# Three operations of VectorE issued later in the order: a weight sum, a product of norm weights, and the transposes of the keys

## The chip, the core and the metric

The kernel runs on one core of one Trainium2 chip. The core has TensorE (PE, the matrix engine; PEld is its weight load), VectorE (DVE), ScalarE (ACT), GpSimd (POOL) and SyncE (SP, which here only issues transfers), and DMA engines that move data between HBM and SBUF. Each engine works through one queue of instructions in order; an instruction that waits holds up everything behind it in its queue. The metric is the device time of one execution in microseconds (us), as the median of several runs.

## What is computed

The reference is a decoder trunk of two layers on 256 tokens with model width 2048 and feed-forward width 8192. Layer 0 mixes tokens with gated linear attention, layer 1 with sliding-window attention over keys and values that are computed once between the layers. Both layers end in an MLP with a squared ReLU.

```python
def sqrelu_mlp(h, w1, w2):
    u = jax.nn.relu(h @ w1)
    return (u * u) @ w2

def shared_kv(h, g_kv, w_k, w_v, g_k):
    u = rmsnorm(h, g_kv)
    k = rmsnorm((u @ w_k).reshape(B, S, SWA_KV_HEADS, SWA_HEAD_DIM), g_k)
    v = (u @ w_v).reshape(B, S, SWA_KV_HEADS, SWA_HEAD_DIM)
...
def swa_sink_mixer(h, k_band, v_band, w_q, g_q, sinks, w_o):
    q = (h @ w_q).reshape(B, S, SWA_KV_HEADS, SWA_GROUP, SWA_HEAD_DIM)
    q = rmsnorm(q, g_q) * (SWA_HEAD_DIM ** -0.5)
```

The keys' norm weight `kv_g_k` and the queries' norm weight `b_g_q` only ever meet as a product, which the kernel forms once (`gkq`) and multiplies into the keys.

## The kernel before

**Matrix products.** Every float32 operand is split into two halves: a rounded half (`wh` for weights, made by ScalarE, line 116) and the rest (`wl`, made by VectorE as `ws - wh`, line 117). A product of a 128x128 block is three matmuls: high by high, high by low, low by high. The function `halve` makes four `wh`/`wl` k-blocks of a 512x512 weight piece in two ScalarE and two VectorE instructions of 128x1024. There are four buffers of `wh` (two k-blocks each), three of `wl` and three of `ws`, the landing place of a weight piece of 1 MB. VectorE comes after ScalarE for each half, and TensorE after VectorE.

**The order of the queues.** The kernel is written as a program in one order; the compiler fills each engine's queue. An instruction's number is its place in the program, and of the instructions that are ready an engine gets the one with the lowest number. `tc.high_priority(offset=WPRI)` gives an instruction a number 60 lower, so that weight loads, halves and weight sums move ahead of their place. The helpers `later(n, fn)` and `tick()` are a clock in the program: `fn` is written n ticks later, and a tick passes about every 12 matmuls.

**The MLP's second product.** For three or four of the four groups of hidden columns (g), `seven` (line 712) computes two times two blocks of 512 columns with Strassen-like sums: seven products in place of eight. It runs for n = 0 and n = 1 in each of seven groups, thus 14 times. The steps that matter here, with the lines:

- `x` and `y` are weight blocks in buffers of their own (783, 791). `y` is block (1,1).
- `plain(2, 1, "E", "F")` (790) multiplies the block (2,1) into two accumulation banks, E for the first 128 tokens and F for the second. Both banks come from the pool `ms`, which has two. At n = 0 they were last used by the first product (`gemm_wide`), whose sums are read out in lines 838 and 839; line 843 applies the ReLU, 844 squares, 847 and 848 split the result.
- `product("E", 2, y)` (792) halves `y` and multiplies.
- Lines 793 to 795 load block (0,1) as `b12` and add it to `y` on VectorE: the last weight sum of the quarter.
- `plain(3, 1, "E", "F")` (796), the sums of E and F into `x12` and `x22` (797, 798), `product("D", 4, x)` (799), a transfer that accumulates onto `x` (`more`, 800, issued by GpSimd), a sum (801).
- `product("C", 6, y)` (802) halves the summed `y` and multiplies: the first user of the sum.
- `plain` of the blocks (2,0) and (3,0), `product("D", 5, x)`, and then in the same manner `b21` added to `x` in line 813.

**Between the layers.** When the last MLP columns of layer 0 are done, four groups of transposes (`operands`, line 614; PE line 610) turn the residual stream into the operands of the key/value product and the query product, with ScalarE in line 241 and VectorE in line 242; `rstd_of` (644) sums the squares. They are written at ticks 0 to 3 around the start of the key/value product. GpSimd meanwhile makes masks (885 to 898) and fetches the two norm weights into `gk` (903, 904). VectorE multiplies them into `gkq` (906). The key/value product (950) is 96 matmuls with a tick after every 12. Its result is normalised (`evac_kv`, 934), multiplied by `gkq` (942), split in two halves (945, 946), and 16 transposes on TensorE with four ScalarE copies (`flip`, 926) bring the keys into `kh` and `kl`; these are written 2 and 3 ticks after the key/value product's end, among the first query product's matmuls (1056).

Of the kernel before, what the change touches and what calls it, by code (L numbers as in the profile page):

```python
# [12 lines left out]
ALU = mybir.AluOpType  # L13
# [18 lines left out]
HD = 64  # L32
NEG = -1.0e30
WS = 3
WHL = 4
WPRI = 60
# [12 lines left out]
def yoco_kernel(ctx: ExitStack, tc: tile.TileContext, x, norms, mlp_w1, mlp_w2, a_w_in, w_glr, w_gate, a_g_o, a_w_o,  # L49
                kv_w_k, kv_w_v, kv_g_k, b_w_q, b_g_q, b_sinks, b_w_o, out):  # L50
    nc = tc.nc
# [4 lines left out]
    wp = ctx.enter_context(tc.tile_pool(name="wp", bufs=2))  # L56
# [14 lines left out]
    def later(n, fn):  # L71
        due.setdefault(now[0] + n, []).append(fn)

    def tick():
        now[0] += 1
        for fn in due.pop(now[0], ()):
            fn()

    def mm(o, l, r, start=True, stop=True, **kw):
        nc.tensor.matmul(o, lhsT=l, rhs=r, start=start, stop=stop, **kw)  # L80
# [23 lines left out]
    def halve(ws, o=C, n=2, between=None):  # L104

        whs = [wp.tile([P, 2, C], F32R, name="wh", tag="wh", bufs=WHL) for _ in range(2)]
        wl = wp.tile([P, 4, C], F32R, name="wl", tag="wl", bufs=WS)
        with tc.high_priority(offset=WPRI):
            for k in range(0, 4, n):
                wh = whs[k // 2]  # L110
                js, ks = slice(k % 2, k % 2 + n), slice(k, k + n)
                with ExitStack() as order:
                    if between:
                        for ins in between(k):
                            order.enter_context(tc.issue_after(ins.ins))
                    h = nc.scalar.copy(out=wh[:, js, :o], in_=ws[:, ks, :o])  # L116
                    l = nc.vector.tensor_sub(out=wl[:, ks, :o], in0=ws[:, ks, :o], in1=wh.bitcast(F32)[:, js, :o])  # L117
                if between:
                    last[:] = h, l
        return [(whs[k // 2][:, k % 2], wl[:, k]) for k in range(4)]  # L120
# [550 lines left out]
    def mlp(w1, w2, act, r, gains):  # L671
# [40 lines left out]
        def seven(w, n, op, us, g, final, acts, gains, sq, nr):  # L712
# [6 lines left out]
            def block(i, j):  # L719
                return w[i * C:(i + 1) * C, (c0 + j) * C:(c0 + j + 1) * C]  # L720

            def load(pool, tag, bufs, i, j):
                ws = pool.tile([P, 4, C], F32, name=tag, tag=tag, bufs=bufs)
                with tc.high_priority(offset=WPRI):
                    nc.sync.dma_start(out=ws, in_=block(i, j).rearrange("(k p) n -> p k n", p=P))
                return ws

            def more(ws, i, j):
                with tc.high_priority(offset=WPRI):
                    nc.gpsimd.dma_start(out=ws, in_=block(i, j).rearrange("(k p) n -> p k n", p=P), accum_op=ALU.add)  # L730
# [3 lines left out]
            def use(b):  # L734
                if b in banks:
                    return banks[b], False
                banks[b] = bank([P, C], {"D": "tp", "E": "ms", "F": "ms"}.get(b, "acc"))
                return banks[b], True

            def product(b, o, ws):  # L740
                p, st = use(b)
                halves = halve(ws)
                for k in range(4):
                    wh, wl = halves[k]
                    mm(p, op[o][:, 0, k], wh, st and k == 0, False, skip_group_check=True)
                    mm(p, op[o][:, 0, k], wl, False, False, skip_group_check=True)
                    mm(p, op[o][:, 1, k], wh, False, k == 3, skip_group_check=True)
                tick()
                return p

            def plain(i, j, b0, b1, apart=False):

                halves = split_w([block(i, j)])
                ah, al, _ = us[i]
                ps_ = [use(b) for b in (b0, b1)]
                order = [(k, t) for k in range(4) for t in range(NT)]
                for n, (k, t) in enumerate(sorted(order, key=lambda kt: kt[1]) if apart else order):
                    wh, wl = halves[k]
                    p, st = ps_[t]
                    tt = slice(t * P, (t + 1) * P)  # L760
                    mm(p, ah[:, k, tt], wh, st and k == 0, False, skip_group_check=True)
                    mm(p, ah[:, k, tt], wl, False, False, skip_group_check=True)
                    mm(p, al[:, k, tt], wh, False, k == 3, skip_group_check=True)
                    if n % 4 == 3:
                        tick()
# [18 lines left out]
            p = product("A", 0, x)  # L784
# [5 lines left out]
            plain(2, 1, "E", "F")  # L790
            y = load(mp, "wy", 1, 1, 1)
            product("E", 2, y)
            b12 = load(wp, "ws", WS, 0, 1)
            with tc.high_priority(offset=WPRI):
                nc.vector.tensor_add(out=y, in0=y, in1=b12)  # L795
            plain(3, 1, "E", "F")
            add(x12, banks["E"])
            add(x22, banks["F"])
            p = product("D", 4, x)
            more(x, 1, 1)  # L800
            add(x21, p)
            sub(x22, product("C", 6, y))
            for i in (2, 3):
                plain(i, 0, "A", "C", i == 2)
# [67 lines left out]
    def last_x(c, b, mp):  # L872

        if b == 0:
# [27 lines left out]
    gk = sp.tile([P, 2, HD], F32, name="gk")  # L902
    nc.gpsimd.dma_start(out=gk[:, 0], in_=kv_g_k.rearrange("(o n) -> o n", o=1).broadcast_to([P, HD]))
    nc.gpsimd.dma_start(out=gk[:, 1], in_=b_g_q.broadcast_to([P, HD]))
    gkq = sp.tile([P, 1, HD], F32, name="gkq")
    nc.vector.scalar_tensor_tensor(out=gkq[:, 0], in0=gk[:, 0], scalar=HD ** -0.5, in1=gk[:, 1], op0=ALU.mult,
                                   op1=ALU.mult)

    def rows(m, n):
        return m.rearrange("p (o n) -> p o n", o=1).broadcast_to([P, n, P])  # L910
# [15 lines left out]
    def flip(src, n, dst):  # L926

        for i in range(0, n, 4):
            tp = bank([P, 4, P], "tp", F32R)
            for j in range(4):  # L930
                nc.tensor.transpose(out=tp[:, j, :], in_=src(i + j), identity=identr)  # L931
            nc.scalar.copy(out=dst(i), in_=tp.bitcast(F32))

    def evac_kv(t, acc):
        a = acc.rearrange("p (h d) -> p h d", d=HD)
        rq = head_norm(a[:, 0:4], 4, t)
        rq = rq.rearrange("p (n o) -> p n o", o=1).broadcast_to([P, 4, HD])
        kn = s2.tile([P, 4, 1, HD], F32, name="kn", tag="kn")
        nc.vector.scalar_tensor_tensor(out=kn[:, :, 0], in0=a[:, 0:4], scalar=rstd[:, t:t + 1], in1=rq, op0=ALU.mult,
                                       op1=ALU.mult)  # L940
        nc.scalar.activation(out=vv[:, t], in_=a[:, 4:8], func=AF.Copy, scale=rstd[:, t:t + 1])
        nc.vector.tensor_mul(out=kn[:, :, 0], in0=kn[:, :, 0], in1=gkq.broadcast_to([P, 4, HD]))
        khl = s2.tile([P, 2, 4, 2, HD], F32R, name="khl", tag="qhl")
        kn2 = kn.broadcast_to([P, 4, 2, HD])
        nc.scalar.copy(out=khl[:, 0], in_=kn2)
        nc.vector.tensor_sub(out=khl[:, 1], in0=kn2, in1=khl.bitcast(F32)[:, 0])
        later(2 + t, lambda: flip(lambda i: khl[:, i // 4, i % 4].rearrange("p a d -> p (a d)"), 8,
                                  lambda i: (kh, kl)[i // 4][:, :, t]))

    go_all(gemm_mov(lambda kq: [kv_w_k[kq * C:(kq + 1) * C, :], kv_w_v[kq * C:(kq + 1) * C, :]], actk, evac_kv))  # L950
# [154 lines left out]
```

## Time and profile before

| | |
|---|---|
| median of 3 runs | 2090.39 us (2089.78 to 2093.33) |
| profiled execution, own time | 2090.28 us |
| its span, first to last instruction | 2088.6 us |
| mean granted TensorE clock | 0.997 |
| VectorE busy | 1428.7 us, 1624 instructions |
| ScalarE busy | 1146.7 us, 1560 instructions |
| GpSimd busy | 177.0 us, 179 instructions |

How to read it: a row of the timeline is a start in us, a duration, the engine, the line, the operation, what it writes and reads, and the number of instructions merged; in square brackets stands how long the engine sat idle before and what ended it. Durations overlap a little with the next instruction, so the distance of two starts is what an instruction costs in a full queue. Of the windows, the last columns are the granted TensorE clock as a share of full speed, the share of the DMA engines, and GB/s. In the view of waits the columns are total us, times, and the longest.

### The profile page before, as it was taken

The page shows a single profiled execution, that of the slowest core. Times are in us where ns is not written, and L with a number is a line of the kernel's source. Part 1 is how long each engine was busy: PE and PEld are TensorE (multiplying, and loading weights), DVE is VectorE, ACT ScalarE, POOL GpSimd, SP SyncE. Part 2 cuts the span into 40 slices and gives each one's busy share as a digit, 9 for nine tenths or more (in the row PEclk, how much of TensorE's full clock was granted, in tenths as well). Part 3 has the DMA queues.
Part 4 walks back from the last instruction along what each step waited for, and adds up shares of the span by engine and source line. Part 5 has one row for each costly group of instructions (what it writes and reads, how often), then busy time and mean ns, then how long its engine had stood idle before and what let it go on. Part 6 is the DMA issues. An engine that isn't in the chain of part 4 may idle for free.

```text
span 2088.6 us, 26959 instructions
## 1 busy us (share of the span) xinstructions
PE 2056.3 (98%) x10734; PEld 1738.8 (83%) x10734; DVE 1428.7 (68%) x1624; ACT 1146.7 (55%) x1560; POOL 177.0 (8%) x179
## 2 busy tenths in 40 slices
PE   9999999999999999999999999999999999999999
PEld 8988888888888788888877777788788888888888
DVE  6696444567866876786797666656776786787554
ACT  6745445555655555554565676455555555555543
POOL 2262111000000000000001232000000000000000
PEclk9999999999999999999999999999999999999999
DMA  8445555656865785776675443655785686676553
GB/s 278 142 142 180 175 174 176 230 190 189 242 231 189 211 270 184 213 240 213 199 193 157 158 141 112 221 188 185 208 271 184 190 255 222 182 225 198 182 192 130
DMA packets 210654, 410.55 MB, mean 197 GB/s; under 512 B 7024, under 2 KB 15232, under 8 KB 210528
## 3 DMA queue, kind: packets, MB, share of 16 engines
q1 hardware_dynamic: 194704, 377.51, 53.8%
q0 software_dynamic: 15104, 30.23, 8.4%
q8 instruction: 84, 1.38, 0.3%
q10 hardware_dynamic: 720, 1.09, 0.2%
q14 instruction: 42, 0.34, 0.0%
HBM read 406.71 MB, written 2.10 MB: 196 GB/s over the span
## 4 chain that ended last, share of the span: by engine, by line
PE 88%; DVE 7%; ACT 3%; issue 1%; DMA 1%; POOL 0%; SPq 0%; ACTq 0%; POOLq 0%; DVEq 0%
PE acc L80 55%; PE ms L80 19%; PE tp L80 13%; DVE wl L117 3%; ACT sc L998 1%; ACT wh L116 1%; PE tp L610 1%; DVE wy L795 1%; DVE m L839 0%; PE tp L931 0%; DVE st L992 0%; DMA ws<-in_a_w_in_dram 0%; DVE st L994 0%; DMA gk<-in_b_g_q_dram 0%; PE tp L559 0%
## 5 line engine op out<-in xcount | busy, mean ns | idle before, releaser
L117 DVE TENSOR_TENSOR wl<-ws,wh 128x1024 fp32r<-128x1024 f32 (+1 forms) x636 | 780.0, 1234 | 472.5 <-ACT wh L116 467.7
L116 ACT CAST wh<-ws 128x1024 fp32r<-128x1024 f32 (+1 forms) x636 | 659.4, 1040 | 577.0 <-PE acc L80 387.6
L80 PE MATMUL acc<-wh,act 128*128 128x512 f32 x1792 | 575.5, 395 | 0.1
L80 PE MATMUL acc<-act,wh 128*128 128x512 f32 (+1 forms) x1664 | 414.1, 362 | 2.2 <-ACT wh L116 1.4
L80 PEld LDWEIGHTS acc<-wh,act 128*128 128x128 f32 x1792 | 336.2, 188 | 73.0 <-issue 3.6
L80 PE MATMUL acc<-wl,act 128*128 128x512 f32 x896 | 349.8, 391 | 0.0
L80 PEld LDWEIGHTS acc<-act,wh 128*128 128x128 f32 x1664 | 278.9, 190 | 29.7 <-ACT wh L116 1.6
L80 PE MATMUL acc<-act,wl 128*128 128x256 f32 x1408 | 257.6, 282 | 0.6 <-DVE wl L117 0.6
L80 PEld LDWEIGHTS acc<-act,wl 128*128 128x128 f32 x1408 | 227.0, 190 | 26.2 <-DVE wl L117 1.0
L80 PE MATMUL tp<-act,wh 128*128 128x512 f32 x592 | 230.1, 394 | 0.0
L80 PE MATMUL ms<-act,wh 128*128 128x512 f32 x576 | 225.9, 394 | 0.0
L80 PEld LDWEIGHTS acc<-wl,act 128*128 128x128 f32 x896 | 168.8, 188 | 35.3 <-issue 1.7
L117 DVE TENSOR_TENSOR wl<-wx,wh 128x1024 fp32r<-128x1024 f32 x112 | 135.9, 1223 | 73.1 <-ACT wh L116 71.2
L116 ACT CAST wh<-wx 128x1024 fp32r<-128x1024 f32 x112 | 117.7, 1055 | 94.3 <-PE acc L80 52.4
L80 PE MATMUL ms<-act,wl 128*128 128x256 f32 x576 | 148.6, 281 | 0.0
L80 PE MATMUL tp<-act,wl 128*128 128x256 f32 x576 | 148.3, 280 | 0.0
L80 PE MATMUL ms<-wh,act 128*128 128x512 f32 x448 | 146.0, 394 | 0.9
L730 POOL DMA_DIRECT2D wx<-in_mlp_w_dram x28 | 36.1, 1289 | 1128.4 <-DVE wl L117 1026.7
L80 PEld LDWEIGHTS tp<-act,wh 128*128 128x128 f32 x592 | 111.5, 189 | 13.3
L80 PEld LDWEIGHTS ms<-act,wh 128*128 128x128 f32 x576 | 108.6, 189 | 13.6
L80 PEld LDWEIGHTS tp<-act,wl 128*128 128x128 f32 x576 | 108.3, 189 | 12.7
L80 PEld LDWEIGHTS ms<-act,wl 128*128 128x128 f32 x576 | 108.5, 189 | 11.9
(231 smaller groups left out, 2242.9 us busy)
## 6 DMA issues: line engine op xcount, KB each, us to landing
ws<-in_mlp_w_dram SPq DMA_DIRECT2D x228, 1024.0 KB, 5.2
ws<-in_a_w_in_dram SPq DMA_DIRECT2D x44, 1024.0 KB, 5.1
wx<-in_mlp_w_dram POOLq DMA_DIRECT2D x28, 1024.0 KB, 8.9
ws<-in_a_w_o_dram SPq DMA_DIRECT2D x16, 1024.0 KB, 5.0
ws<-in_b_w_q_dram SPq DMA_DIRECT2D x16, 1024.0 KB, 5.0
ws<-in_b_w_o_dram SPq DMA_DIRECT2D x16, 1024.0 KB, 5.0
wx<-in_mlp_w_dram SPq DMA_DIRECT2D x14, 1024.0 KB, 5.1
wy<-in_mlp_w_dram SPq DMA_DIRECT2D x14, 1024.0 KB, 7.5
```

Source lines behind the costliest of these rows:

```text
L80: nc.tensor.matmul(o, lhsT=l, rhs=r, start=start, stop=stop, **kw)
L116: h = nc.scalar.copy(out=wh[:, js, :o], in_=ws[:, ks, :o])
L117: l = nc.vector.tensor_sub(out=wl[:, ks, :o], in0=ws[:, ks, :o], in1=wh.bitcast(F32)[:, js, :o])
L610: nc.tensor.transpose(out=tp[:, j, t], in_=xs[c][:, t, (2 * b + j) * P:(2 * b + j + 1) * P], identity=ident)
L730: nc.gpsimd.dma_start(out=ws, in_=block(i, j).rearrange("(k p) n -> p k n", p=P), accum_op=ALU.add)
L795: nc.vector.tensor_add(out=y, in0=y, in1=b12)
L998: nc.scalar.activation(out=sc[:, h], in_=sc[:, h], func=AF.Exp, bias=nmx[:, h:h + 1], scale=f[:, h:h + 1], accum_out=su[:, h:h + 1])
```

## The change

Three places are written later in the program; no instruction is added, removed or made different.

- In `seven`, the load of `b12` and its sum into `y` move from before `plain(3, 1)` to just before `product("C", 6, y)`: behind 36 matmuls, two sums and the halves of two weight pieces in the written order, still with the 60 of `WPRI`.
- `gkq` is written at the fourth tick of the key/value product instead of before it.
- The keys' transposes are written 5 and 6 ticks after the key/value product instead of 2 and 3.

```diff
             y = load(mp, "wy", 1, 1, 1)
             product("E", 2, y)
-            b12 = load(wp, "ws", WS, 0, 1)
-            with tc.high_priority(offset=WPRI):
-                nc.vector.tensor_add(out=y, in0=y, in1=b12)
             plain(3, 1, "E", "F")
             add(x12, banks["E"])
             add(x22, banks["F"])
             p = product("D", 4, x)
             more(x, 1, 1)
             add(x21, p)
+            b12 = load(wp, "ws", WS, 0, 1)
+            with tc.high_priority(offset=WPRI):
+                nc.vector.tensor_add(out=y, in0=y, in1=b12)
             sub(x22, product("C", 6, y))
...
     gkq = sp.tile([P, 1, HD], F32, name="gkq")
-    nc.vector.scalar_tensor_tensor(out=gkq[:, 0], in0=gk[:, 0], scalar=HD ** -0.5, in1=gk[:, 1], op0=ALU.mult,
-                                   op1=ALU.mult)
+    later(4, lambda: nc.vector.scalar_tensor_tensor(out=gkq[:, 0], in0=gk[:, 0], scalar=HD ** -0.5, in1=gk[:, 1],
+                                                    op0=ALU.mult, op1=ALU.mult))
...
-        later(2 + t, lambda: flip(lambda i: khl[:, i // 4, i % 4].rearrange("p a d -> p (a d)"), 8,
+        later(5 + t, lambda: flip(lambda i: khl[:, i // 4, i % 4].rearrange("p a d -> p (a d)"), 8,
                                   lambda i: (kh, kl)[i // 4][:, :, t]))
```

## The prediction

> **What bounds the kernel now.** I read the page's busy shares first, then the waits of TensorE, then the timelines around them.
>
> ```profile
> PE 2056.3 (98%) x10734; PEld 1738.8 (83%) x10734; DVE 1428.7 (68%) x1624; ACT 1146.7 (55%) x1560; POOL 177.0 (8%) x179
> ```
> ```profile
> PE ms L80 <- DVE wl L117: 9.0, 8, 1.2
> PE tp L610 <- DVE rv L644: 4.5, 1, 4.5
> ...
> PE tp L931 <- ACT khl L945: 2.0, 1, 2.0
> ```
>
> TensorE is busy for 2056.3 of 2088.6 us, so nothing here is worth more than its 32 us of holes and the matmuls that run slowly beside them. Three of its longest waits lie at the places that the change touches: eight of about 1.1 us for a low weight half, one of 4.5 at the transposes between the layers, and one of 2.0 at the keys' transposes. I take them in turn.
>
> **The weight sum at n = 0.** There are 14 sums; the first lies at 514.60, and this is VectorE's, ScalarE's and TensorE's timeline around it:
>
> ```profile
> L795 DVE TENSOR_TENSOR wy<-wy,ws x14: 2283/2286/2291, 514.6 to 1867.6; 128x2048 f32<-128x2048 f32 x14
> ```
> ```profile
> 511.40 0.41 DVE L839 TENSOR_TENSOR m<-tp,m 128x256 f32<-128x256 f32 x1
> 511.73 2.35 DVE L117 TENSOR_TENSOR wl<-wy,wh 128x1024 fp32r<-128x1024 f32 x2
> 514.00 0.69 DVE L843 SCALAR_TENSOR_TENSOR m<-m,rb 128x512 f32<-128x512 f32 x1
> 514.60 2.29 DVE L795 TENSOR_TENSOR wy<-wy,ws 128x2048 f32<-128x2048 f32 x1
> 516.80 0.69 DVE L848 TENSOR_TENSOR act<-u,act 128x512 fp32r<-128x512 f32 x1
> 517.40 2.36 DVE L117 TENSOR_TENSOR wl<-ws,wh 128x1024 fp32r<-128x1024 f32 x2
> 519.67 0.42 DVE L839 TENSOR_TENSOR m<-ms,m 128x256 f32<-128x256 f32 x1
> ```
> ```profile
> 510.25 0.40 ACT L838 COPY m<-ms 128x256 f32<-128x256 f32 x1
> 515.95 1.06 ACT L116 CAST wh<-ws 128x1024 fp32r<-128x1024 f32 x1
> 517.31 1.05 ACT L116 CAST wh<-ws 128x1024 fp32r<-128x1024 f32 x1 [0.30 <-PE ms L80]
> ```
> ```profile
> 511.54 0.50 PE L80 MATMUL ms<-wh,act 128*128 128x512 f32 x1
> 514.39 0.39 PE L80 MATMUL ms<-wh,ops 128*128 128x512 f32 x1
> 517.11 0.44 PE L80 MATMUL ms<-wh,act 128*128 128x512 f32 x1
> 518.68 0.50 PE L80 MATMUL ms<-wl,act 128*128 128x512 f32 x1 [1.12 <-DVE wl L117]
> 527.16 0.39 PE L80 MATMUL tp<-wh,op 128*128 128x512 f32 x1
> ```
>
> TensorE begins `plain(2, 1)` at 511.54 and does its bank E, 12 matmuls, then product E. The 12 of bank F are not done then, for F is the bank that the fourth sum of line 839 still has to read, and VectorE comes to that one only at 519.67, though ScalarE's part of it was over at 510.65. In VectorE's queue it stands behind the weight sum and behind the two halves of `plain(3, 1)`, all three of which were given lower numbers by the 60. So at 517.11 TensorE has only `plain(3, 1)` to go on with, whose low half isn't there: it waits until 518.68, and after six matmuls again for the bank.
>
> What that costs is the distance from 517.11 to the next product at 527.16, 10.05 us, less the matmuls in it:
>
> ```profile
> L80 PE MATMUL ms<-wh,act 128*128 128x512 f32 x24 | 7.9, 397 | 0.1
> L80 PE MATMUL ms<-wl,act 128*128 128x512 f32 x12 | 4.8, 399 | 1.1 <-DVE wl L117 1.1
> ```
> ```profile
> 527.32 2.72 PE tp L80 x12
> ```
>
> 12 matmuls in a row take 2.72 us, or 0.227 each; 36 take 8.16. The loss is 1.89 us for each of the seven groups, 13.2 in all.
>
> With the change the weight sum's number lies 39 matmuls and sums further back, behind line 839. After line 843, at 514.60, the read-out of bank F is the lowest number that is ready: it takes 0.33 (the step from 511.40 to 511.73), and F is free at about 515. TensorE, in the middle of product E, then has the 12 matmuls of F in hand, 2.72 us, and reaches `plain(3, 1)` at 514.39 + 24 x 0.227 = 519.84 instead of 517.11; it wants the first low half 0.23 later, at 520.07. VectorE can even put the weight sum into the same place as before: 514.60 + 0.33 + 0.60 (line 843 again) = 515.53, sum to 517.73 (2.20, the step from 514.60 to 516.80), line 848 to 518.33, low half to 519.55. That is half a microsecond early. In the five groups that are not the first of their layer a sum into `v` (0.6) comes in as well, and the half is 0.1 late. From there on TensorE runs 1.9 us ahead of before, and VectorE, whose rows above leave no hole from 511.40 to 520, has to keep up; I leave 0.3 of the loss standing: 1.6 x 7 = **11.2 us**, with 13.2 as the one bound and nothing as the other. A loss is the rival below.
>
> Moved with the sum is the load of `b12`. It now takes its `ws` buffer after `plain(3, 1)`; a later load waits for the buffer that the sum releases:
>
> ```profile
> SPq L130 <- DVE wy L795: 70.0, 13, 5.8
> ```
> ```profile
> ws<-in_mlp_w_dram SPq DMA_DIRECT2D x228, 1024.0 KB, 5.2
> ```
>
> The load behind it (block (3,0)) then waits for the halves of `plain(3, 1)` instead, which end at 519.76, and lands 5.2 later at 525; TensorE comes to the block after products D and C and the block (2,0), at 527.16 + 48 x 0.227 = 538. `b21`, released by the sum itself, is wanted after another 24 matmuls and a product. I cost the loads at nothing: some 10 us of matmuls hide them. GpSimd's accumulating transfer keeps its place.
>
> **The weight sum at n = 1.** No read-out lies in its way here.
>
> ```profile
> 554.79 2.35 DVE L117 TENSOR_TENSOR wl<-wy,wh 128x1024 fp32r<-128x1024 f32 x2
> 557.18 2.29 DVE L795 TENSOR_TENSOR wy<-wy,ws 128x2048 f32<-128x2048 f32 x1
> ...
> 566.53 1.22 DVE L117 TENSOR_TENSOR wl<-wy,wh 128x1024 fp32r<-128x1024 f32 x1 [0.75 <-ACT wh L116]
> 567.67 1.28 DVE L767 TENSOR_TENSOR xs<-ms,xs 128x512 f32<-128x512 f32 x2
> ```
> ```profile
> 557.28 1.06 ACT L116 CAST wh<-ws 128x1024 fp32r<-128x1024 f32 x1 [1.17 <-PE ms L80]
> ```
> ```profile
> 570.68 0.39 PE L80 MATMUL acc<-wh,op 128*128 128x512 f32 x1
> ```
>
> At 557.18 the next half is not ready (its `wh` ends at 558.34), so the sum, which is ready, probably goes at the same moment as before. TensorE doesn't wait here now: 0. Of the eight waits in the table, one is at n = 1 of the last group of layer 0, where VectorE is busy for nearly all of 22 us:
>
> ```profile
> 1074.00:1096.00 22.00, 20.58 (x95) 16.35 (x94) 21.91 (x30) 16.39 (x30) 1.31 (x2) 1.00 0.81 208
> ```
>
> A sum that is moved inside a full queue only moves the wait: 0, between -1.2 and +1.2.
>
> **The product of the norm weights.** The profile's rows around it:
>
> ```profile
> 1123.78 0.47 ACT L241 ACTIVATE act<-tp,gT 128x256 fp32r<-128x256 f32 x1
> ...
> 1129.87 0.23 DVE L906 SCALAR_TENSOR_TENSOR gkq<-gk 128x64 f32<-128x64 f32 x1 [5.07 <-DMA gk<-in_b_g_q_dram]
> 1130.01 0.87 DVE L242 SCALAR_TENSOR_TENSOR act<-tp,gT,act 128x256 fp32r<-128x256 f32 x2
> 1130.86 1.22 DVE L117 TENSOR_TENSOR wl<-ws,wh 128x1024 fp32r<-128x1024 f32 x1
> ```
> ```profile
> 1131.03 0.63 PE L610 MATMUL tp<-ident,xs 128*128 128x128 f32 x4 [4.48 <-DVE rv L644]
> ```
> ```profile
> 1131.00:1135.00 4.00, 3.98 (x13) 3.23 (x14) 4.00 (x7) 2.31 (x4) 1.64 (x1) 0.57 0.13 8
> ```
>
> VectorE stands for 5.07 us until the second norm weight has landed. Behind it wait two operand halves (the first had its input at 1124.25), the sum of squares and the first low half of the third weight piece; TensorE, whose next transposes want that bank, stands for 4.48, and for the 4 us after it the granted clock is 0.57, another 4.00 x 0.43 = 1.7. Together 6.2. [...]
>
> Four ticks later the product's number lies behind the transposes' operands and the sum of squares. I expect those ahead of it, which frees the bank. The norm weight still lands at 1129.8, and the low half may still stand behind the product: done at 1129.87 + 0.14 + 1.22 = 1131.2, while TensorE, going on at 1126.5 with 4 transposes (about 0.4) and the 12 matmuls that it has halves for (2.72), wants it 0.23 later, at 1129.9. About 1.4 stay, too short for the slow stretch (beside the wait of 1.2 between 1074 and 1096 the clock is 1.00): 6.2 - 1.4 = **4.8 us**. The bounds are 0 (the queue doesn't change) and 6.2. The product's user, line 942, comes 20 us later.
>
> **The keys' transposes.**
>
> ```profile
> 1158.48 0.62 ACT L945 CAST khl<-kn 128x512 fp32r<-128x512 f32 x1 [0.99 <-DVE kn L942]
> ```
> ```profile
> 1159.15 0.54 PE L931 MATMUL tp<-identr,khl 128*128 128x128 f32 x4 [1.98 <-ACT khl L945]
> ```
>
> TensorE waits 1.98 for the keys' halves, which are ready at 1159.1; three ticks are 36 matmuls or 8.2 us, so the wait goes. The four ScalarE copies move with them, hidden by an engine that is busy 55% of the time; `kh` is first read in the next query product, three ticks after the first one's eight, so 5 ticks (13.6 us) behind the last of the transposes. **2.0 us**, between 0 and 2.2.
>
> **The sum.** 11.2 + 4.8 + 2.0 = 18.0 us. The profiled execution took 2090.28, the median of the runs is 0.1 above it: 2090.4 - 18.0 = **2072.4 us**.
>
> **Rivals.**
> *The norm product stays where it is.* The half at 1130.01 belongs to the first group of transposes, which is written before the product: it had the lower number already, its input came at 1124.25, and the product passed it all the same. So the compiler filled the queue as if nothing else had been ready at 1124.8, and a number decides only among the ready. If the product is taken in the same hole again, 4.8 is missing: 2077.2. Against it: at the fourth tick more operations have the lower number. Chance 0.27, against 0.42 for the forecast.
> *The weight sum brings nothing.* If TensorE's order keeps `plain(3, 1)` ahead of bank F, it waits at 517.11 as before, since ScalarE's `wh` ends at 517.01 and the low half at 518.2 at the earliest: 0.4 a group at best. Then 2090.4 - 4.8 - 2.0 = 2083.6. Chance 0.13.
> *The change doesn't do what it says*: all ready operations go as before, at most the transposes move: 2088 to 2090. Chance 0.09.
> *The sum comes too late (slower).* Product C needs sum, ScalarE's half (1.06) and the low half (1.22) one after the other. At n = 1 TensorE wants the low half at 570.91, so the sum must begin by 566.3. If it is queued behind the two bank sums that end at 568.95, the half is done at 568.95 + 2.29 + 1.06 + 1.22 = 573.5, 2.6 late. Over 14 sums that is 36 us, and 2072.4 + 36 = 2108. For it speaks that the sum's number is now next to product C's; against it, that the sum is ready from 557.14 on and the half next to it not before 558.34. Chance 0.07. The 0.02 left lie between these.
>
> **The numbers.** About 0.2% (4 us) can be told from no change. Faster by more are the forecast and the first two rivals, with a little of the rest: 0.84; the same 0.09; slower 0.07. All bounds at their best give 13.2 + 6.2 + 2.2 = 21.6, or 2068.8; up to the second rival it is 2083.6. The range from 2068.5 to 2084 holds 0.42 + 0.27 + 0.13 = 0.82.
>
> **What would show it.** Right: the fourth read-out of line 839 ahead of the weight sum at n = 0, bank F's matmuls before product E ends, TensorE's waits for low halves at one instead of eight; no row of 0.57 after 1126; no wait at line 931. Wrong: the sum's row directly ahead of ScalarE's half of `wy` with TensorE waiting at product C, or line 906 again with 5 us of idle time before it and TensorE with 4.5.

## The result, and the profile after

| | before | after |
|---|---|---|
| median of 4 runs each, same chip | 2091.14 us (2089.78 to 2093.33) | 2066.77 us (2066.42 to 2068.05) |
| ratio, 95% interval | | 0.9887 (0.9874 to 0.9900) |
| profiled execution, own time | 2090.28 us | 2066.73 us |
| its span | 2088.6 us | 2065.0 us |

The change is faster by 24.4 us by the medians and by 23.55 by the two profiled executions. The forecast was 18.0, and the measured time lies 1.7 us below the low end of the range. The page's busy shares and TensorE's waits after:

```profile
PE 2047.3 (99%) x10734; PEld 1737.6 (84%) x10734; DVE 1427.5 (69%) x1624; ACT 1143.6 (55%) x1560; POOL 176.8 (9%) x179
```
```profile
PE tp L931 <- ACT po L1015: 3.6, 3, 1.2
PE acc L80 <- ACT wh L116: 2.6, 2, 2.4
PE tp L1012 <- DVE pv L1020: 2.4, 2, 1.8
PE ms L80 <- POOL ones L88: 1.2, 1, 1.2
PE tp L80 <- DVE act L242: 1.1, 1, 1.1
```

The rows of 9.0, 4.5 and 2.0 us are gone. Those of lines 1015 and 1012 stood in the kernel before as well. The 2.4 for a high half lies at 7.6 us, in the start. The last row is new: all eight waits for a low half in the banks of `ms` are gone, and one of 1.12 us has come in at n = 1 of the last group of layer 0:

```profile
1081.40 2.29 DVE L801 TENSOR_TENSOR wy<-wy,ws 128x2048 f32<-128x2048 f32 x1
1083.60 0.87 DVE L242 SCALAR_TENSOR_TENSOR act<-tp,gT,act 128x256 fp32r<-128x256 f32 x2
```
```profile
1084.22 0.47 PE L80 MATMUL tp<-wh,op 128*128 128x512 f32 x1 [1.12 <-DVE act L242]
```

Product D wants a bank that line 242 has yet to read, and line 242 stands behind the weight sum in VectorE's queue. It is the pattern of bank F once more, at another place and with another read-out.

VectorE and TensorE of the first group at n = 0, after:

```profile
513.84 0.69 DVE L843 SCALAR_TENSOR_TENSOR m<-m,rb 128x512 f32<-128x512 f32 x1
514.44 0.42 DVE L839 TENSOR_TENSOR m<-ms,m 128x256 f32<-128x256 f32 x1
514.78 2.28 DVE L801 TENSOR_TENSOR wy<-wy,ws 128x2048 f32<-128x2048 f32 x1
516.98 0.69 DVE L848 TENSOR_TENSOR act<-u,act 128x512 fp32r<-128x512 f32 x1
```
```profile
511.38 0.50 PE L80 MATMUL ms<-wh,act 128*128 128x512 f32 x1
...
515.18 0.39 PE L80 MATMUL ms<-wl,ops 128*128 128x512 f32 x1
515.41 0.39 PE L80 MATMUL ms<-wh,act 128*128 128x512 f32 x1
...
517.90 0.39 PE L80 MATMUL ms<-wh,act 128*128 128x512 f32 x1
518.13 0.62 PE L80 MATMUL ms<-wh,ops 128*128 128x512 f32 x2
...
525.19 0.39 PE L80 MATMUL tp<-wh,op 128*128 128x512 f32 x1
```

The fourth read-out of line 839 stands at 514.44, directly ahead of the weight sum, which keeps its old place at 514.78 (514.60 before). TensorE has the 12 matmuls of bank F in hand at 515.41, in the middle of product E (`ops`), as the forecast had it. From the first matmul of `plain(2, 1)` to product D pass 525.19 - 511.38 = 13.81 us; before it was 527.16 - 511.54 = 15.62. That is 1.81 less.

The norm weights and the keys, after:

```profile
1116.57 0.56 POOL L904 DMA_DIRECT2D gk<-in_b_g_q_dram  x1
1117.00 0.15 DVE L644 TENSOR_REDUCE rv<-sq 128x2 f32<-128x8 f32 x1
1119.66 0.60 PE L610 MATMUL tp<-ident,xs 128*128 128x128 f32 x4
```
```profile
1125.68 0.21 DVE L906 SCALAR_TENSOR_TENSOR gkq<-gk 128x64 f32<-128x64 f32 x1
```
```profile
1147.43 0.80 PE L931 MATMUL tp<-identr,khl 128*128 128x128 f32 x8
1150.89 0.80 PE L931 MATMUL tp<-identr,khl 128*128 128x128 f32 x8
```

No idle time is left ahead of any of them. The second norm weight takes 5.5 us from issue to landing, so it is there at about 1122; the product comes 3.6 us later.

Where the time went, by the same instruction's start in both profiles:

| instruction | before | after | difference | gained since the row above |
|---|---|---|---|---|
| first `plain(2, 1)` | 511.54 | 511.38 | -0.16 | 0.16 (start) |
| first product D | 527.16 | 525.19 | -1.97 | 1.81 |
| sum into `x`, line 813, last group of layer 0 | 1108.64 | 1100.54 | -8.10 | 6.13: three groups at n = 0 (5.46) and n = 1 of the last (0.67) |
| sum of squares of the keys, line 920 | 1148.89 | 1134.55 | -14.34 | 6.24 |
| first halves of the queries, line 961 | 1173.23 | 1156.61 | -16.62 | 2.28 |
| line 1002, last attention group | 1305.37 | 1288.69 | -16.68 | 0.06 |
| line 626, first output sum behind the attention | 1327.89 | 1309.52 | -18.37 | **1.69** |
| end | 2088.6 | 2065.0 | -23.6 | 5.23 (three groups at n = 0) |

The row in bold is at a place that the change doesn't touch. The work there and TensorE's two waits (1.81 and 0.57 us before, 1.79 and 0.57 after) are the same in both; TensorE's granted clock (the third column from the right) isn't. Before, and then after:

```profile
1308.00:1312.00 4.00, 1.63 (x10) 0.98 (x9) 4.00 (x6) 1.04 (x1) 0.00 (x0) 1.00 0.16 29
1312.00:1316.00 4.00, 4.00 (x13) 1.02 (x11) 1.92 (x2) 0.59 (x1) 0.00 (x0) 0.57 0.83 264
```
```profile
1291.30:1295.30 4.00, 1.65 (x10) 1.00 (x9) 4.00 (x6) 1.05 (x2) 0.00 (x0) 1.00 0.20 32
1295.30:1299.30 4.00, 4.00 (x20) 2.16 (x19) 2.47 (x3) 1.66 (x3) 0.00 (x0) 1.00 0.77 260
```

Behind the hole in which TensorE waits for the masks of the last attention group (line 1020), the kernel before runs 3.4 us at half clock, which costs 1.7; the changed kernel runs on at full clock.

### The profile page after: what moved, and what is told of

It reads as the page before. It is cut to its first block, busy times and chain, and to the rows that moved or that the text cites. A ratio compares the mean times of both kernels' runs of the same rounds, so it can differ in the third digit from the quotient of the medians.

```text
span 2065.0 us, 26968 instructions
## 1 busy us (share of the span) xinstructions
PE 2047.3 (99%) x10734; PEld 1737.6 (84%) x10734; DVE 1427.5 (69%) x1624; ACT 1143.6 (55%) x1560; POOL 176.8 (9%) x179
## 4 chain that ended last, share of the span: by engine, by line
PE 92%; DVE 4%; ACT 2%; DMA 1%; issue 1%; SPq 0%; POOL 0%; ACTq 0%; POOLq 0%; DVEq 0%
PE acc L80 57%; PE ms L80 21%; PE tp L80 13%; DVE wl L117 1%; ACT sc L998 1%; PE tp L610 1%; ACT wh L116 1%; PE tp L931 0%; DMA xt<-in_x_dram 0%; DMA ws<-in_a_w_in_dram 0%; DVE st L992 0%; DVE st L994 0%; DVE act L242 0%; PE tp L559 0%; DVE po L1020 0%
```

## The experiments

All times are medians; each group is compared with runs of the kernel before on the same chip (2090.3 to 2091.6).

**The weight sum alone.** The first hunk of the diff, applied to the kernel before.

```diff
             product("E", 2, y)
-            b12 = load(wp, "ws", WS, 0, 1)
-            with tc.high_priority(offset=WPRI):
-                nc.vector.tensor_add(out=y, in0=y, in1=b12)
...
             add(x21, p)
+            b12 = load(wp, "ws", WS, 0, 1)
+            with tc.high_priority(offset=WPRI):
+                nc.vector.tensor_add(out=y, in0=y, in1=b12)
```

> The kernel before with the weight sum moved and nothing else. Theory A (the sum had the read-out of bank F behind it): 1.8 us in each of the seven groups at n = 0, thus 12.5, and 0.7 at n = 1 of the last group of layer 0: 2091.1 - 13.2 = 2077.9. The seven waits of 1.12 us for a low half in the second block's matmuls are gone, those of 4.48 (line 644) and 1.98 (line 945) stay. Rival B (the three parts help one another, the sum alone is worth less than in the whole change): 11.2 or less, 2080 or above. How the slow-clock stretches fall adds or takes 1.7 in single executions under either.

2077.73 us against 2090.77, ratio 0.9937 (0.9925 to 0.9949): 13.0 gained (10.7 to 15.7), and the waits of 4.5 and 2.0 us stay. Theory A. The times alone would leave rival B's 11.2 just possible; the rows don't: line 813 of the last group of layer 0 starts at 1100.51, 8.13 earlier than before, against 8.10 in the whole change. So the part is worth alone what the table above gives it within the whole. The profiled run, at 2079.16 the slowest of the five, has half clock for 6.8 us around the stall of the norm weights (1121.77 to 1128.60) and for 3.4 behind the keys' wait (1152.49 to 1155.91), where the kernel before has 3.4 and none.

**The read-out ahead, the sum left in place.** In the kernel before, lines 838 and 839 of the last piece get numbers 60 lower.

```diff
+                    with ExitStack() as first:
+                        if seven_of and c == NC4 - 1 and f >= 2:
+                            first.enter_context(tc.high_priority(offset=WPRI))
-                    nc.scalar.copy(out=m[:, j], in_=acc[:, 1])
+                        nc.scalar.copy(out=m[:, j], in_=acc[:, 1])
...
```

> The kernel before, the weight sum in its old place in the program; instead the read-outs of the third and fourth sums (lines 838, 839) of the last first-product piece get numbers 60 lower, so that the read-out of bank F stands ahead of the weight sum in VectorE's queue. Theory A (what cost the time is that read-out behind the sum): the same 12.5 us at n = 0 as by moving the sum, 2078.6, and bank F's matmuls inside product E. Rival B (the later place of the sum itself helps, since the low halves of the next block come sooner): no gain, 2091.

2082.04 against 2090.77, ratio 0.9957 (0.9945 to 0.9970): 8.7, between the two. VectorE and TensorE of this kernel (its lines behind 835 are numbered 3 higher, the sum is 795):

```profile
513.50 0.42 DVE L842 TENSOR_TENSOR m<-ms,m 128x256 f32<-128x256 f32 x1
513.83 2.28 DVE L795 TENSOR_TENSOR wy<-wy,ws 128x2048 f32<-128x2048 f32 x1
516.03 0.68 DVE L846 SCALAR_TENSOR_TENSOR m<-m,rb 128x512 f32<-128x512 f32 x1
```
```profile
511.04 0.50 PE L80 MATMUL ms<-wh,act 128*128 128x512 f32 x1
...
520.62 0.50 PE L80 MATMUL ms<-wh,act 128*128 128x512 f32 x1 [0.21 <-DVE act L851]
...
525.29 0.39 PE L80 MATMUL tp<-wh,op 128*128 128x512 f32 x1
```

The read-out stands ahead of the sum as in the changed kernel, and the group takes 525.29 - 511.04 = 14.25 us, 1.37 less than before: three quarters of the 1.81 come from bank F being free, without the sum moving. Most of the missing 0.44 lies at a small wait, 0.21 here and seven times in the kernel, for the operands that the ReLU (line 843, here 846) leads to: the step across it, 520.02 to 520.62, is 0.60 where a matmul takes 0.23.

> As bank_first, and the ReLU and the square of the same pair (lines 843 and 844) get the lower numbers too. Theory A (bank_first lacked some 0.4 us a group, because the ReLU came behind the weight sum and TensorE waited 0.2 for the second operand half): the 12.5 us in full, 2078.3, within 1 us of the moved sum. Rival B (the moved sum has a merit of its own, such as the later load): again 8 to 10, 2081 to 2082.

With the ReLU and the square raised too (the `with` reaches down to line 844), it is 2082.21 against 2091.41, ratio 0.9956 (0.9943 to 0.9970): 9.2, no better. The explanation by the ReLU falls. There is again a small wait in seven places, now for ScalarE's operand half: 1.3 us in all, longest 0.2. In both kernels the last 0.4 a group is missing where TensorE waits for an operand half that one of these two engines makes late; which order of the operand halves and the weight halves would mend it, these runs don't show.

**The product of the norm weights.** Three kernels from the kernel before: the product at tick 4, at tick 1 and at tick 2 (`later(4, ...)`, `later(1, ...)`, `later(2, ...)`, as in the second hunk of the diff).

> The kernel before with the product of the norm weights at the fourth tick and nothing else. Theory A (it comes long after its data, and the whole wait with the slow stretch behind it goes): 6.2 us, 2084.9, no wait for line 644 and no window with half clock around 1130. Rival B (the forecast's step: the weights still land too late and 1.4 stay): 4.8 us, 2086.3, with a wait of TensorE of about 1.4.

2084.52 against 2090.77, ratio 0.9969 (0.9957 to 0.9980): 6.25 (4.2 to 9.0). The times alone don't decide between 6.2 and 4.8; the profile does, for no wait of TensorE is left there, and from line 813 to line 922 pass 34.48 us in place of 40.75, 6.27 less: the whole stall with its half clock. The weight is issued at 1124.35 and lands 5.2 later, at 1129.55; the product comes at 1133.45 without a wait. Half clock hasn't left this kernel, though: it now stands behind the keys' wait, from 1152.98 to 1156.40, where the kernel before had none.

> The kernel before with the product of the norm weights at the first tick in place of the fourth: in VectorE's queue it then stands right behind two more operand halves and the sum of squares, some 2 us later than before, still ahead of the landing of its data. Theory A (a wait in the queue only has to let the work pass that TensorE wants next): the operands of the first transposes pass, but the halves of two weight pieces stand behind the product; TensorE's wait is 1 to 2.5 us in place of 4.48, and too short for the slow stretch: 3.5 to 5 us gained, about 2086.7. Rival B (any place that still waits for the landing costs the same, since all later work is behind it): 0 to 1, 2090 or above.

2090.97 against 2090.31, ratio 1.0000 (0.9991 to 1.0009): nothing. VectorE and TensorE of this kernel:

```profile
1125.13 0.15 DVE L644 TENSOR_REDUCE rv<-sq 128x2 f32<-128x8 f32 x1
1129.83 0.23 DVE L906 SCALAR_TENSOR_TENSOR gkq<-gk 128x64 f32<-128x64 f32 x1 [4.55 <-DMA gk<-in_b_g_q_dram]
1129.97 0.87 DVE L242 SCALAR_TENSOR_TENSOR act<-tp,gT,act 128x256 fp32r<-128x256 f32 x2
1130.60 0.85 PE L610 MATMUL tp<-ident,xs 128*128 128x128 f32 x4 [3.81 <-DVE act L242]
```

The sum of squares and two operand halves have passed the product; VectorE still stands 4.55 us, and TensorE wants the two operand halves behind it. The wait is 3.81 in place of 4.48 and has another name. Rival B. That a wait of 1 to 2.5 us is too short for the slow stretch was the author's estimate; this kernel had no such wait.

> The kernel before with the product of the norm weights at the second tick: behind the next two operand halves and the low halves of two weight pieces, at about 1128.1, 1.5 us ahead of its data. Theory A (what counts is how long VectorE still stands, and whether TensorE wants what is behind it): VectorE stands 1.5, the next two operand halves come 1.9 late, TensorE's transposes behind them have slack of some us: 5.5 to 6.2 gained, about 2085. Rival B (all or nothing: any wait for the landing costs the whole): 0 to 1, 2090.

2084.79 against 2091.41, ratio 0.9963 (0.9951 to 0.9976): 6.6. VectorE, and the transposes on TensorE:

```profile
1126.00 0.87 DVE L242 SCALAR_TENSOR_TENSOR act<-tp,gT,act 128x256 fp32r<-128x256 f32 x2
...
1126.85 1.22 DVE L117 TENSOR_TENSOR wl<-ws,wh 128x1024 fp32r<-128x1024 f32 x1
1127.99 0.87 DVE L242 SCALAR_TENSOR_TENSOR act<-tp,gT,act 128x256 fp32r<-128x256 f32 x2
1129.62 0.22 DVE L906 SCALAR_TENSOR_TENSOR gkq<-gk 128x64 f32<-128x64 f32 x1 [0.76 <-DMA gk<-in_b_g_q_dram]
```
```profile
1127.20 0.60 PE L610 MATMUL tp<-ident,xs 128*128 128x128 f32 x4
```

Now two more pairs of operand halves and two low halves have passed the product, VectorE stands only 0.76, and that costs nothing. What lies between tick 1 and tick 2 is the pair of operand halves that TensorE's next transposes wait for: here it stands at 1126.00, ahead of the product, and the transposes follow at 1127.20 without a wait; at tick 1 it stands behind the product, at 1129.97.

**The weights early, the product in place.** The two loads go ahead of the first MLP, into a lasting buffer; the other queues are untouched.

```diff
+    gk = const.tile([P, 2, HD], F32, name="gk")
+    nc.gpsimd.dma_start(out=gk[:, 0], in_=kv_g_k.rearrange("(o n) -> o n", o=1).broadcast_to([P, HD]))
+    nc.gpsimd.dma_start(out=gk[:, 1], in_=b_g_q.broadcast_to([P, HD]))
     (actk, actq), rstd = mlp(mlp_w1[0], mlp_w2[0], actm, rm, (G_KV, G_MIX1))
...
-    gk = sp.tile([P, 2, HD], F32, name="gk")
-    nc.gpsimd.dma_start(out=gk[:, 0], in_=kv_g_k.rearrange("(o n) -> o n", o=1).broadcast_to([P, HD]))
-    nc.gpsimd.dma_start(out=gk[:, 1], in_=b_g_q.broadcast_to([P, HD]))
```

> The kernel before, the product of the norm weights in its old place in every queue, but the two loads of the norm weights issued before the first MLP, some 600 us earlier, into a buffer that lasts. The queues of TensorE, VectorE, ScalarE and SyncE are the same as before, GpSimd's alone has the loads elsewhere. Theory A (the wait is for the transfer alone, its place in VectorE's queue does no harm once the data is there): the 5.07 us of VectorE and the 4.48 of TensorE go with the slow stretch, 6.2 us, 2084.9. Rival B (something else was late there too, such as GpSimd's masks or the sum of squares): 3 or less, 2088 or above.

2084.88 against 2090.31, ratio 0.9971 (0.9959 to 0.9982): 5.4 to 6. The product then stands at 1124.29 without a wait. So the stall was the transfer, and the place in the queue does harm only while the data is missing.

**The keys' transposes alone** (third hunk of the diff).

> The kernel before with the keys' transposes three ticks later and nothing else. Theory A: the wait of 1.98 and its shadow go, 2.3 us, 2088.8. Rival B (the transposes' own place later makes the first score product wait): 1 or less, 2090 or above. Slow-clock stretches that fall or do not fall behind the last attention group make 1.7 in single executions, as much as the effect.

2087.95 against 2090.77, ratio 0.9984 (0.9975 to 0.9993): 2.8. The 16 transposes wait for nothing. Its runs lie in two groups, four at 2085.5 to 2086.3 and seven at 2087.5 to 2089.5: that is more of a spread than the effect. The rows give it more closely: from line 922 to line 962 pass 22.16 us in place of 24.47, 2.31 less. The profiled run, of 2088.72, has lost some of it again ahead of that, with half clock for 6.8 us around the stall of the norm weights (1129.92 to 1136.74) in place of 3.4.

**The slower rival, brought about.** In the changed kernel the sum is held behind the sum of bank F.

```diff
-            add(x22, banks["F"])
+            behind = add(x22, banks["F"])
...
-            with tc.high_priority(offset=WPRI):
+            with tc.high_priority(offset=WPRI), tc.issue_after(behind.ins):
                 nc.vector.tensor_add(out=y, in0=y, in1=b12)
```

> The changed kernel with the weight sum held behind the sum of bank F (line 798) on VectorE in all 14 places: the slower rival of the prediction, made on purpose. Theory A (product C then needs sum, ScalarE's half and the low half one after the other): 2.4 to 2.6 us at each of 14 places, about 34, 2101, with TensorE waiting for halves of wy at product C. Rival B (there is slack that the rival did not see): 2067 to 2072.

2113.29 us, 46 above the changed kernel and slower than before: 1.0105 (1.0091 to 1.0119). TensorE's two longest waits:

```profile
PE acc L80 <- ACT wh L116: 21.1, 15, 1.5
PE acc L80 <- DVE wl L117: 10.8, 15, 0.8
```

At the first place TensorE waits 1.42 for the high half of `wy` and 0.76 for the low one, 2.2 in all. 14 such places make most of the 31.9 us of the two rows. The expectation lacked the clock: six of these waits have a stretch of half clock behind them, which begin at 531.0, 575.4, 711.9, 756.3, 1114.7 and 1548.2, at some 1.7 us each. So the rival's mechanism and place were right, and its price of 36 us was too low.

**The hole behind the last attention group.** TensorE waits there for masks (line 1020) that stand in VectorE's queue behind two low halves. In the kernel mask_first the last group's mask products get numbers 60 lower, on top of the change; before_mask does the same to the kernel before.

```diff
-                for o, m in ((po, ownT), (pv, prevT)):
-                    nc.vector.tensor_mul(out=o, in0=tp, in1=rows(m, 4))
+                with ExitStack() as first:
+                    if g == 3:
+                        first.enter_context(tc.high_priority(offset=WPRI))
+                    for o, m in ((po, ownT), (pv, prevT)):
+                        nc.vector.tensor_mul(out=o, in0=tp, in1=rows(m, 4))
```

> The changed kernel, and in the last attention group the four mask products (line 1020) get numbers 60 lower, so that they stand ahead of two low halves in VectorE's queue, behind which they stood as bank F's read-out stood behind the weight sum. Theory A (same mechanism): TensorE's waits of 1.79 and 0.57 before the transposes of line 1012 go, 2.4 us less or 1.9 if a half comes later, 2064.6, and with the hole the chance of a slow-clock stretch behind it, so that the spread of the runs falls from 1.6 us to 0.5 or less. Rival B (the low halves that are now later are wanted at once): no gain, 2067.

2064.62 us (2064.24 to 2067.88), ratio to before 0.9878 (0.9865 to 0.9892): by the medians 2 to 3 us better than the changed kernel, 2.15 against its first and 3.07 against its second (below), though the intervals of the ratios overlap (0.9874 to 0.9900 for the first). The profile shows the hole gone: the four mask products stand together (line 1020 is 1023 here), and TensorE's row for line 1012 and `pv` is no longer there:

```profile
1292.72 0.64 DVE L1023 TENSOR_TENSOR po<-tp,ownT 128x512 f32<-128x512 f32 x1
1293.27 0.68 DVE L1023 TENSOR_TENSOR pv<-tp,prevT 128x512 f32<-128x512 f32 x1
1293.87 0.68 DVE L1023 TENSOR_TENSOR po<-tp,ownT 128x512 f32<-128x512 f32 x1
1294.47 0.68 DVE L1023 TENSOR_TENSOR pv<-tp,prevT 128x512 f32<-128x512 f32 x1
```

Only the spread didn't shrink: the run of 2067.88 lost its time in the start, where its profile has half clock from 17.2 to 24.0 us.

> The kernel before with the mask products of the last attention group ahead of the two low halves, as in mask_first. Theory A (in the kernel before the hole costs its 2.4 and the slow stretch behind it): 4.1 us, 2086.8. Rival B (the hole costs the same 2.2 in both kernels, so the 1.7 came from elsewhere): 2088.7.

2086.50 against 2091.59, ratio 0.9977 (0.9968 to 0.9987), or 4.8 (2.7 to 6.7). That is nearer theory A's 4.1, and the interval lies above the 2.2 of rival B, though not by much. So the hole costs the kernel before more than the 2.4 us of its waits, and what its profile shows besides is the slow stretch.

> The kernel of mask_first, and in the first three attention groups the masks and transposes of the first 128 tokens and the weighted sum one tick later, so that the transposes of the next queries no longer want a bank that ScalarE has yet to read out (line 1015). Theory A: three waits of 1.2 go, 3.6 us less than mask_first, 2061.0. Rival B (the banks collide at the next tick instead): 2064 to 2066.

One step further (`ATT = (5, 3), (11, 8), (12, 10)`) it is 2065.71 (2065.65 to 2065.94), not 2061: the waits for line 1015 are gone, but TensorE now waits in three places for scores (line 983), 1.2 us in all, and 0.8 for a mask. Rival B: by the ratios, 0.9876 against 0.9878, it is no faster than mask_first.

**Whose doing the missing 1.7 us is.**

> The changed kernel once more, word for word, for the 1.7 us that its first profile lacks behind the last attention group. Theory A (the slow-clock stretch comes when an edge of a fixed grid of 3.413 us falls between 0.4 before and 0.75 after the second group of transposes behind the hole, whatever the kernel): its times fall into two groups some 1.7 apart, about 2066.6 and 2068.2, and this profile has half clock near 1295 just when its edges fall so. Rival B (the change itself took the stretch away): no execution has it, all within 0.5 of 2066.6 but for the start.

The changed kernel again: 2067.69 (2066.70 to 2068.43), ratio 0.9885 (0.9871 to 0.9898). Its times do fall into two groups, but not for the reason given: the profile, of a run of 2068.43, has full clock at the hole, and the 1.7 lie far ahead of it: the hole comes at 1295.66 in place of 1293.93, and the first read-out of line 839 that stands at 510.57 in the first profile already comes at 512.35. What theory A rests on is the profile of before, in steps of 0.1 us:

```profile
1131.50:1131.60 0.10, 0.10 (x3) 0.10 (x2) 0.10 (x1) 0.00 (x0) 0.00 (x0) 0.71 0.00 0
1134.90:1135.00 0.10, 0.10 (x2) 0.10 (x1) 0.10 (x1) 0.00 (x0) 0.00 (x0) 0.73 2.91 102
1312.40:1312.50 0.10, 0.10 (x3) 0.10 (x4) 0.10 (x1) 0.00 (x0) 0.00 (x0) 0.73 1.16 451
1315.80:1315.90 0.10, 0.10 (x2) 0.00 (x0) 0.00 (x0) 0.00 (x0) 0.00 (x0) 0.70 0.65 246
```

These are the edges of the two slow stretches: 0.71 means half clock in 0.06 of the 0.1. They lie at 1131.54, 1134.95, 1312.45 and 1315.86. A stretch lasts 3.41, and the two begin 180.91 apart, 53 steps of 3.413. The half clock in the start of the same execution begins at 8.56, which is 329 such steps ahead of 1131.54.

> The changed kernel with 9 extra matmuls of 0.227 us, whose result nobody reads, at the end of the key/value product: all that follows comes 2.04 us later. Theory A (the slow-clock stretch behind the last attention group depends only on where a fixed grid of 3.413 us meets the hole; in the two profiles of the changed kernel the nearest edges lie 0.85 to 1.25 before and 2.2 to 2.6 after the second transposes, outside the interval from -0.4 to +0.75): 2.04 us move an edge to 0.1 to 0.5, and the stretch is there, 2.04 + 1.7 = 3.7 us, 2070.9 against 2067.2 for the two medians of the changed kernel. Rival B (the stretch has left with the change): 2.04, 2069.2, and no window of half clock after 1290.

2068.58 us (2068.38 to 2069.44).

> As fill9 with 15 extra matmuls, 3.41 us, one whole step of the grid. Theory A: the edges meet the hole as in the changed kernel, no stretch: 3.4 us, 2070.6, no more than with 9. Rival B: 3.4 as well, but 1.4 more than fill9.

2070.61 us (2069.48 to 2071.60). Neither kernel tests what it was meant to: the compiler laid the first five of the extra matmuls at 1126 to 1129, ahead of the place meant, and the hole didn't move by the intended amount. The edges miss it in both profiles, with no slow stretch, as theory A has it for such edges; but B has it too.

The next three kernels put the extra matmuls elsewhere:

```diff
+    def extra():
+        o = small()
+        for i in range(9):
+            mm(o, identr, acta[1][2][:, 3].rearrange("p a t -> p (a t)"))
     for g in range(4):
+        if g == 3:
+            later(7, extra)
```

> The changed kernel with 9 extra matmuls of 0.227 us, whose result nobody reads, in a row within the query product of the fourth attention group, where TensorE has no hole to hide them: all that follows comes 2.04 us later. Theory A (a fixed grid of 3.413 us; the stretch comes when an edge falls from 0.4 before to 0.75 after the second transposes of the hole): edges that stood 2.2 to 2.6 after them now stand 0.2 to 0.6 after them, half clock there, 2.04 + 1.7: 3.7 above the changed kernel, 2070.9. Rival B (the stretch has left with the change): 2.04 above, 2069.2, no half clock after 1290.

> As extra9 with 11 extra matmuls, 2.50 us. Theory A: edges from 0.3 before to 0.1 after the second transposes, half clock there: 4.2 above the changed kernel, 2071.4. Rival B: 2.5 above, 2069.7.

> As extra9 with 15 extra matmuls, 3.41 us, one whole step of the grid. Theory A: the edges meet the hole as in the changed kernel, no half clock there: 3.4 above, 2070.6, that is less than extra11 though it computes more. Rival B: 3.4 above too, 0.9 more than extra11.

The diff is that of extra9; the others have 11 and 15 in the loop. The matmuls stand in a row from 1249 on. 9 give 2069.36 (2068.42 to 2070.50), 11 give 2070.24 (2068.38 to 2070.55), 15 give 2069.94 (2068.39 to 2070.25). With 11 the stretch is back (clock, 1296 to 1300 and 1300 to 1304):

```profile
1296.00:1300.00 4.00, 3.31 (x12) 1.68 (x14) 3.44 (x4) 0.00 (x0) 0.00 (x0) 0.66 0.84 262
1300.00:1304.00 4.00, 4.00 (x17) 2.42 (x14) 0.69 (x1) 1.66 (x3) 0.00 (x0) 0.91 0.82 262
```

With 9 it isn't there and with 15 it is, against what was expected: TensorE's wait of 1.19 at line 931 behind them took up part of the delay (it is gone in these three profiles), and the start of an execution shifts all by up to 1.7 us (the hole at 1295.66 in after_again, at 1293.93 in after), so the edges didn't fall where they were meant to. But each profile shows its own edges; where the hole has no stretch, they are an estimate, carried forward in steps of 3.4133 from the half clock in the first 13 us (in extra15, which shows both, 7.46 to 1297.70 is 378 such steps). In all 17 profiles with this hole, counted from the start of the second transposes (1311.80 before), the twelve with an edge from -0.42 to +0.83 us have the stretch; the five with the nearest edges at -0.85, -0.86, -1.14, +1.27 and +1.36 have none. B falls: two profiles of the changed kernel with nothing but matmuls added have the stretch. Theory A fits all 17 profiles, but its interval is read off these same profiles, and two of the three placements came out other than expected. Why all nine profiles of the kernel before and its variants fell into the interval, and three of eight from the changed one, stays open; by chance alone an interval of 1.3 in 3.41 would take three or four of nine. A phase fixed to the start isn't the reason: the edges of the nine lie between 0.1 and 2.7 us into a step counted from the first instruction.

## Why the prediction was too slow

The mechanism was right at all three places; the time came out below the range because one gain lies where the forecast counted nothing, and because each of the three terms was counted too low.

- **Weight sum, n = 0: 12.5 for a forecast of 11.2.** The read-out ahead of the sum, the place of the sum, and bank F's matmuls within product E came as said; only the second row of line 843, which the forecast had ahead of the sum, came behind it (517.58). The step that failed is "I leave 0.3 of the loss standing": 0.08 stands (1.89 less 1.81), for VectorE kept up.
- **n = 1: 0.67 for 0.** In the last group of layer 0, "a sum that is moved inside a full queue only moves the wait" held by the letter: the wait of 1.16 for a low half became one of 1.12 at product D (1084.22), whose bank line 242 had yet to read. A second wait of the kernel before, 0.27 for a low half of `wy` at 1092.48, went as well; the rest of the 0.67 these rows don't place. It lay within the bound of 1.2, but the sum of the bounds left it out.
- **Norm weights: 6.24 for 4.8.** The step that failed is that "the low half may still stand behind the product" with 1.4 of wait left. The product was taken to stay among the next operations; it stands thirteen instructions behind the sum of squares in VectorE's queue, 3.6 us after its data. Tick 2 shows that even 0.76 of wait there costs nothing, and tick 1 that the rival's fear was fair: three ticks earlier this part would have brought nothing. The stretch of half clock was rightly counted to the stall (34.48 us from line 813 to line 922 in gkq_only, 40.75 before). That it would go with a wait of 1.4 left no run shows: in gkq_only it went with no wait left.
- **Keys: 2.28 for 2.0**, above the bound of 2.2. The term took the wait of 1.98 alone; the step across it, from the last matmul at 1156.79 to the transposes at 1159.15, was 2.36 where a matmul takes 0.23, thus 2.13 lost.
- **The attention: 1.7 for nothing.** The forecast looked for half clock where the change is. It read 0.57 at 1131 and passed over the same 0.57 at 1312, where the hole is 1.8 and 0.6 us; "too short for the slow stretch", said of a wait of 1.4, was an estimate from one wait of 1.2 beside a clock of 1.00, and no run shows how short is short enough. The step that failed is "all bounds at their best give 21.6", which bounded only the touched places: a shift of the whole program brought or took a stretch of 1.7 at the hole behind the attention, and behind the keys' wait in sum_only and gkq_only. The terms as measured, 0.16 + 12.5 + 0.67 + 6.24 + 2.28 + 1.7, make the 23.55. These 1.7 are luck as far as the change goes: nothing in it aims at them, and extra11 and extra15 show that they can come back. Without them the first median would have been about 2068.5, the low end of the range.
- The rivals: the norm product didn't stay, the sum brought nearly all it could, and the slower rival is real but needs the sum to be held: it began at 525.77 in that kernel and at 514.78 in the changed one, where it took its old place directly behind the read-out.

## What to carry to other kernels

When a wait names a weight half or an operand, look which read-out of a bank stands behind the raised work on that engine; raising the read-out or lowering the work both help (here 8.7 and 13.0 us). An operation that waits for a transfer did no harm in VectorE's queue here as long as TensorE wanted nothing behind it before the landing: at tick 2 VectorE stood 0.76 us and 6.6 us were gained, one tick earlier it stood 4.55, TensorE 3.81, and nothing was gained. Before summing the bounds, list every window of low clock in the whole trace, also where the change does nothing: here the hole behind the last attention group, with waits of 1.8 and 0.6 us, had another 1.7 us of half clock behind it in the kernel before and in extra11, and none in the changed kernel.

## What the runs showed of the hardware

Half clock came in stretches of 3.41 us, or two of them on end. In the kernel before three of them begin at 8.56, 1131.54 and 1312.45, which is 329 and then 53 steps of 3.413 apart; in extra15 two begin at 7.46 and 1297.70, 378 steps apart. It came without an idle stretch of that length: in the kernel before, the 3.41 us ahead of the edge at 1312.45, from 1309.04 on, held 0.63 us of transposes and 0.65 of the next, 38% of it work (rows, kernel before):

```profile
1310.60 0.63 PE L1012 MATMUL tp<-ident,sc 128*128 128x128 f32 x4 [1.81 <-DVE pv L1020]
1311.80 0.63 PE L1012 MATMUL tp<-ident,sc 128*128 128x128 f32 x4 [0.57 <-DVE pv L1020]
```

The 3.41 us ahead of the edge at +0.83 (bank_chain) held 43% of work, and half clock followed; those ahead of the estimated edges at -0.85 and -0.86 (fill9, after) held 47%, and it did not. In sum_late the 4 us from 708 to 712 held 1.82 us of work, and the clock of the next 4 is 0.58. What decides whether half clock follows, these runs don't show.

The price of one stall varied from kernel to kernel: half clock around the stall of the norm weights lasted one step, 3.41 us, in the kernel before and at tick 1, and two, 6.8 us, in sum_only, bank_first, bank_chain, keys_only and before_mask. In keys_only the time from line 813 to line 922 is 1.24 us longer than before (41.99 in place of 40.75).
